# All of x ahead of the modulation pieces, filler matmuls around them, later query transposes in a two-layer mixer

## The chip, the cores and the metric

The kernel runs on one core of a Trainium2 chip. The metric is the device time of one execution in microseconds; lower is better.

## The reference

Two layers work on 256 latent tokens (x) and 256 context tokens, 2048 wide, in float32. Each layer computes shift, scale and gate from a conditioning vector, normalizes, projects, mixes in three ways, and adds the gated result:

```python
for l in range(2):
    shift, scale, gate = split(silu(c) @ ada_w[l] + ada_b[l], 3)        # 2048 -> 6144
    h = rmsnorm(x, norm_g[l]) * (1 + scale) + shift                     # context: its own vector c_ctx
    q, k, v, u_pool, u_fourier, g = split_proj(h @ w_in[l])             # 2048 -> 4608
    q = rope(rmsnorm(q)); k = rope(rmsnorm(k))                          # 8 query heads, 2 key heads
    mixed = concat(attention(q, k, v), pool(u_pool), fourier(u_fourier))
    x = x + gate * ((mixed * silu(g)) @ w_out[l])
return rmsnorm(x, final_norm_g)
```

## The kernel before

Tokens lie along the free dimension and channels along the partitions: x is loaded as 16 blocks of 128 channels by 512 tokens, in four groups of four blocks (`load_x`, L114). A large product in float32 is done by splitting both factors into a rounded part and a remainder (`split`, L137 to 139: ScalarE casts `hi`, VectorE subtracts for `lo`) and three matmuls of 512 columns (`mm3`). Weights come through three buffers of each of `raw`, `whi` and `wlo` (`wpiece`, L142), so a fourth weight piece waits until the first one's `lo` is made. All loads are issued on one queue, SP, in order.

**The startup** (`startup`, L838) makes the first layer's shift and scale and the normalized input `h` while the first weights arrive. The squares of x are made by ScalarE (three of four blocks) and VectorE (the fourth), summed in pairs by VectorE, and summed over channels by TensorE with a matrix of ones into two PSUM tiles (`stats`, eight matmul rows per half group). `norm` does the fourth group's `stats`, then the square root and the reciprocal (`rstd`). The modulation weights of layer 0 come in ten groups (`GROUPS`), for one or two channel blocks each, and each group in up to four pieces (`piece`, 512 KB or 1 MB, through four buffers). `ada_part` multiplies a piece with the conditioning vector, eight rows each; after the last piece of a group ScalarE copies the result (`ev`), TensorE transposes it, VectorE reduces it and makes `ab` and from it `h` (`make_h`). Behind each piece `work` issues matmuls of the projection from a list whose weights and `h` are there. `warm(n)` issues n float32 matmuls of ones with no use of the result (two rows each in the trace). TensorE's instructions in the startup stand in the order of the program. For the rest of the kernel, and for the other engines and SP, a planner orders the instructions by priority and by its own costs.

**The side work** (`Side`) interleaves attention with the projections: each generator yields a cost and a lag, `tick(0.64)` is called behind three matmuls, and a step is taken when the counted time has come. `q_prep` first makes the head norms and the rotary embedding of one 128-token block on VectorE, yields with a lag of 3.0, transposes the block's four heads on TensorE (L525), and goes on to the next block. It is added with a delay of `LAG_E` = 5.6 after each of the two query chunks of a layer, with `attention` behind it.

Of the kernel before, what the change touches and what calls it, by code (L numbers as in the profile page):

```python
# [20 lines left out]
P = 128  # L21
# [25 lines left out]
LAG_S, LAG_T, LAG_E, LAG_Q = 4.3, 1.4, 5.6, 0.0  # L47
# [9 lines left out]
def backbone(  # L57
# [24 lines left out]
    V, S, G, PE = nc.vector, nc.scalar, nc.gpsimd, nc.tensor  # L82
# [13 lines left out]
    def name(s):  # L96
        count[0] += 1
        return f"{s}_{count[0]}"
# [7 lines left out]
    def smt():  # L106
        return sm.tile([P, 512], F32, tag="sm", name=name("sm"))
# [6 lines left out]
    def load_x(g, n):  # L114
        for j in range(0, 4, n):
            nc.sync.dma_start(xk[g][:, j : j + n], xT[:, 4 * g + j : 4 * g + j + n])

    idt = const.tile([P, P], F32, name="idt")
    ones = const.tile([P, P], F32, name="ones")
# [17 lines left out]
    def split(src, hi, lo):  # L137
        i = S.copy(hi, src)  # L138
        V.tensor_sub(lo, src, hi.bitcast(F32))  # L139
        return i  # L140
# [143 lines left out]
    side = Side()  # L284
# [86 lines left out]
    def f4(s, shape, dt=F32R):  # L371
        return late["f4"].tile(list(shape), dt, tag="f4", name=name(s))
# [145 lines left out]
    def q_prep(qraw, qT, rq):  # L518
        rq.append(head_rstd(qraw, 4, P ** -0.5))
        for tt, r in qraw:  # L520
            qo = rope_one(tt, r, 4, 0)
            yield 0.0, 3.0 if tt == 0 else 1.0
            tp = smt()
            for hh in range(4):
                PE.transpose(tp[:, hh * P : hh * P + P], qo[:, hh], idt)  # L525
            c = slice(tt * P, tt * P + P)
            split(tp.rearrange("p (h n) -> p h n", h=4), qT[0][:, :, c], qT[1][:, :, c])
            yield 0.43, 0.0
# [47 lines left out]
    def layer(l, h, xs, chunk0):  # L576
# [62 lines left out]
        for g in range(2):  # L639
            accs = b_chunk(l, 3 + g, h, ntt, FILL[l][2])  # L640
            qraw = evac_raw(accs)
            if l == 0:
                side.finish("a0")
                qT = pair8(4, (T,))
            else:
                qT = [a.rearrange("p a (b n) -> p (a b) n", b=2) for a in pair8(2, (2 * N,))]
            rq = []
            side.add(f"q{g}", q_prep(qraw, qT, rq), LAG_E, "k")
            for qt in range(ntt):
                side.add(f"a{g}", attention(g, qt, qT, rq, kT, vv, mixed, off), 0.0, f"q{g}")  # L650
        korder = list(range(8, 16)) + list(range(8))
# [48 lines left out]
        k = KT - 1  # L700
        ws = [wpiece(wo[k, half], (P, 8, P)) for half in range(2)]
        for s in range(2):
            a = mmt()
            c = slice(s * N, s * N + N)
            for half, (hi, lo) in enumerate(ws):
                for j in range(8):
                    kk = korder[half * 8 + j]
# [121 lines left out]
            V.scalar_tensor_tensor(th, th, 1.0, g, op0=ALU.add, op1=ALU.mult)  # L829
        return th  # L830

    for g in range(3):
        load_x(g, 2)
    cq = [f4("cq", (P, 2, 512), F32) for _ in range(2)]
    h0 = H(T, "h")

# [1 line left out]
    def startup():  # L838
        st = tc.tile_pool(name="st", bufs=ST)
        with st as st:  # L840
# [14 lines left out]
            def stats(g):  # L855
                q = [t2("sq") for _ in range(4)]
                for j in range(4):
                    x = xk[g][:, j]
                    if j == 3:
                        V.tensor_mul(q[j], x, x)  # L860
                    else:
                        i = S.activation(q[j], x, AF.Square)
                        if g == 0 and j == 0:
                            tc.add_manual_dep(
                                i.ins, root.ins.name, mybir.DependencyInfo(mybir.DependencyClass.NoSync, mybir.DependencyReason.DATA)
                            )
                    if j % 2:
                        V.tensor_add(q[j - 1], q[j - 1], q[j])
                pairs = [(o, c, j) for o, c in zip(ss, halves) for j in (0, 2)]
                for o, c, j in pairs if g == 3 else sorted(pairs, key=lambda e: e[2]):  # L870
                    PE.matmul(o[:, :N], ones, q[j][:, c], start=g == 0 and j == 0, stop=g == 3 and j == 2)
# [3 lines left out]
            def norm():  # L875
                stats(3)
                for o, c in zip(ss, halves):
                    S.activation(rstd[:, c], o[:, :N], AF.Sqrt, bias=epst, scale=1.0 / D)
                for c in halves:
                    V.reciprocal(rstd[:, c], rstd[:, c])  # L880
                V.tensor_scalar(adab[:, KT : 2 * KT], adab[:, KT : 2 * KT], 1.0, None, op0=ALU.add)

            first = [mmt() for _ in range(4)]
            early = {}
            gfirst = [smt() for _ in range(NE)]
# [64 lines left out]
            start = [sum(GROUPS[:j]) * P * 4096 for j in range(len(GROUPS))]  # L950
# [28 lines left out]
            def ada_part(a, raw, kk, first_, last, w_):  # L979
                for i in range(4):  # L980
                    PE.matmul(  # L981
                        a[32 * i : 32 * i + 32, :w_], cs[:, 4 * kk + i], raw[:, i], start=first_, stop=last, tile_position=(0, 32 * i)
                    )

            def warm(n):
                for _ in range(n):
                    PE.matmul(first[3][:, :P], ones, ones, start=True, stop=True)

            with tc.manual_schedule(engines={mybir.EngineType.PE}):
                for g in range(3):  # L990
                    stats(g)
                for j, gs in enumerate(GROUPS):
                    a = smt()
                    w_ = 256 * gs
                    npc = 4 - ND[j]
                    raws = []
                    for kk in range(npc):
                        if j == 0 and kk == 1:
                            load_x(3, 1)
                        if j == 1 and kk == 3:  # L1000
                            late["store"]()
                        if kk == npc - 1 and j + 1 < len(GROUPS):
                            dvec(j + 1)
                        raws.append(piece(j, kk))
                        now[0] = 4 * j + kk + 4 - npc
                        if kk + 4 - npc == (PFK if j else 3):
                            queue(4 * j + 4 + (QK if j else Q0), k0, gs)
                        if j == 0 and kk == 2:
                            norm()
                        if j == 0 and kk == 3:  # L1010
                            nc.sync.dma_start(idt, ident)
                        ada_part(a, raws[kk], kk, kk == 0, kk == npc - 1, w_)
                        if j == 1 and kk < 2:
                            warm(3 - 2 * kk)
                        work(RATE * gs // 2)
                    with tc.high_priority(offset=CHAIN if j == 0 else 0):
                        ev = t2("ev")
                        S.copy(ev[:, :w_], a[:, :w_])
                        if j:
                            work(4)  # L1020
                        else:
                            warm(3)
                        for q in range(2 * gs):
                            PE.transpose(a[:, q * P : q * P + P], ev[:, q * P : q * P + P], idt)
                        if j:
                            work(4)
                        else:
                            store_cb(cvk, a[:32, 2 * P : 3 * P])
                            warm(2)
                        red = sp.tile([P, 2, gs, 2], F32, tag="red", name=name("red"))  # L1030
                        V.tensor_reduce(
                            red.rearrange("p w k v -> p (w k) v"), a[:, :w_].rearrange("p (q g r) -> p q r g", g=4, r=32)[:, :, 0:2, :],
                            axis=AX.X, op=ALU.add,
                        )
                        dst = ab[0][:, :, k0 : k0 + gs]
                        bias = adab[:, : 2 * KT].rearrange("p (w k) -> p w k", w=2)[:, :, k0 : k0 + gs]
                        for e in range(ND[j]):
                            V.tensor_add(red, red, abq[:, e, :, k0 : k0 + gs])
                        V.tensor_add(dst, red, bias.unsqueeze(3).to_broadcast([P, 2, gs, 2]))
                        V.tensor_mul(dst[:, 1], dst[:, 1], ng[:, k0 : k0 + gs].unsqueeze(2).to_broadcast([P, gs, 2]))  # L1040
                        for i in range(gs):
                            k = k0 + i
                            for vs in ((0,), (1,)) if k == 0 else ((0, 1),):
                                make_h(h0, k, xk[k // 4][:, k % 4], rstd, 0, vs)
                    k0 += gs
                now[0] = 10 ** 6
                work(LATE)
                pool_tables(0)
                fourier_loads(0)
                work(10 ** 6)  # L1050
                rope_tables(0)
# [131 lines left out]
```

## Time and profile before

| what | us |
|---|---|
| median of 3 runs (1071.56 to 1074.11) | 1073.24 |
| profiled execution, its own time | 1073.19 |
| its span, first to last instruction | 1071.4 |
| TensorE busy in the span | 1047.4 |
| VectorE busy | 842.3 |
| ScalarE busy | 479.7 |

Between the span and the execution's own time lie 1.8 us. Busy time of TensorE counts matmuls from issue to a modelled end, so a full row of it can still hide matmuls further apart than they need be. Times in the rows are microseconds from the start of the span. A chain of waits is followed back from the last instruction: at each step to what released it.

### The profile page before, as it was taken

To read this page: it belongs to the slowest core of one execution; us is meant where nothing else is said; L and a number is where in the kernel's file an instruction comes from. 1 tells how busy PE (TensorE), PEld (TensorE's weight loads), DVE (VectorE), ACT (ScalarE), POOL (GpSimd) and SP (SyncE) were. 2 spreads that over 40 slices of the span, in tenths; PEclk is the share of its full clock that TensorE was granted. 3 is DMA by queue.
4 is the path that set the end of the run, shared out by engine and by line. 5 is a ranking of instruction groups with operands and counts; after the bars stand their busy time and mean duration, and the time that the engine had idled before them with its cause. 6 is when DMAs were issued, how large, how long until landed. Compare 5 with 4: busy or idle time off the path is not lost.

```text
span 1071.4 us, 14049 instructions
## 1 busy us (share of the span) xinstructions
PE 1047.4 (98%) x5100; PEld 842.6 (79%) x5100; DVE 842.3 (79%) x1553; ACT 479.7 (45%) x803; POOL 0.2 (0%) x4
## 2 busy tenths in 40 slices
PE   6899999999999999999999999999999999999996
PEld 4466677888787888888888888887888888888885
DVE  6358648998999779998989787489657889776565
ACT  5233225323323766632522223288326767447453
POOL 0000000000000000000000000000000000000000
PEclk9999999999999999999999999999999999999999
DMA  8999777566785244457776667445764565686563
GB/s 336 410 398 343 256 238 242 164 198 214 227 260 169 80 140 158 157 192 273 266 272 213 197 195 265 139 133 169 271 218 161 168 196 185 224 270 212 192 201 117
DMA packets 63797, 233.63 MB, mean 218 GB/s; under 512 B 7104, under 2 KB 8176, under 8 KB 60016
## 3 DMA queue, kind: packets, MB, share of 16 engines
q1 hardware_dynamic: 63152, 231.69, 63.8%
q10 hardware_dynamic: 576, 1.05, 0.3%
q8 instruction: 40, 0.66, 0.3%
q14 instruction: 29, 0.24, 0.1%
HBM read 230.58 MB, written 2.12 MB: 217 GB/s over the span
## 4 chain that ended last, share of the span: by engine, by line
PE 81%; DVE 7%; DMA 4%; ACT 3%; issue 3%; SPq 0%; DVEq 0%; ACTq 0%
PE mm L336 18%; PE mm L335 18%; PE mm L337 18%; PE mm L932 6%; PE mm L311 5%; PE sm L932 3%; DVE ajunk L188 2%; DMA a<-in_ada 2%; PE mm L312 2%; PE sm L336 2%; PE sm L337 2%; PE sm L335 2%; PE sm L981 2%; DVE wlo L139 2%; PE sm L562 1%
## 5 line engine op out<-in xcount | busy, mean ns | idle before, releaser
L138 ACT CAST whi<-raw 128x1024 fp32r<-128x1024 f32 (+1 forms) x216 | 219.9, 1019 | 333.0 <-PE mm L336 112.1
L139 DVE TENSOR_TENSOR wlo<-raw,whi 128x1024 fp32r<-128x1024 f32 (+1 forms) x216 | 255.3, 1182 | 103.7 <-ACT whi L138 102.6
L188 DVE SCALAR_TENSOR_TENSOR ajunk<-araw,cbt 128x1024 bf16<-128x1024 f32 x224 | 273.6, 1221 | 49.8 <-DMA araw<-in_adar 36.9
L335 PE MATMUL mm<-whi,h 128*128 128x512 f32 x416 | 167.6, 403 | 0.0
L336 PE MATMUL mm<-wlo,h 128*128 128x512 f32 x416 | 163.3, 393 | 0.0
L337 PE MATMUL mm<-whi,h 128*128 128x512 f32 x416 | 163.1, 392 | 0.0
L335 PE MATMUL mm<-m,whi 128*128 128x512 f32 (+1 forms) x272 | 102.6, 377 | 0.0
L336 PE MATMUL mm<-m,whi 128*128 128x512 f32 (+1 forms) x272 | 102.4, 377 | 0.0
L337 PE MATMUL mm<-m,wlo 128*128 128x512 f32 (+1 forms) x272 | 102.4, 377 | 0.0
L311 PE MATMUL mm<-h,whi 128*128 128x512 f32 x256 | 92.5, 400 | 0.0
L337 PEld LDWEIGHTS mm<-whi,h 128*128 128x128 f32 x416 | 78.1, 188 | 17.0 <-DVE h L139 0.3
L336 PEld LDWEIGHTS mm<-wlo,h 128*128 128x128 f32 x416 | 78.2, 188 | 16.2 <-issue 1.9
L335 PEld LDWEIGHTS mm<-whi,h 128*128 128x128 f32 x416 | 78.2, 188 | 16.1 <-issue 1.7
L335 PE MATMUL mm<-h,whi 128*128 128x512 f32 x196 | 77.7, 396 | 0.0
L337 PE MATMUL mm<-h,wlo 128*128 128x512 f32 x196 | 76.8, 392 | 0.0
L336 PE MATMUL mm<-h,whi 128*128 128x512 f32 x196 | 76.8, 392 | 0.0
L312 PE MATMUL mm<-h,wlo 128*128 128x256 f32 x256 | 72.4, 283 | 0.0
L932 PE MATMUL mm<-whi,h 128*128 128x512 f32 x192 | 63.8, 401 | 0.2 <-ACT h L138 0.2
L335 PEld LDWEIGHTS mm<-m,whi 128*128 128x128 f32 x272 | 51.2, 188 | 9.5
L337 PEld LDWEIGHTS mm<-m,wlo 128*128 128x128 f32 x272 | 51.2, 188 | 9.4
L336 PEld LDWEIGHTS mm<-m,whi 128*128 128x128 f32 x272 | 51.2, 188 | 9.2
L311 PEld LDWEIGHTS mm<-h,whi 128*128 128x128 f32 x256 | 48.1, 188 | 10.8
(229 smaller groups left out, 1639.1 us busy)
## 6 DMA issues: line engine op xcount, KB each, us to landing
araw<-in_adar SPq DMA_DIRECT2D x128, 512.0 KB, 4.0
raw<-in_wb SPq DMA_DIRECT2D x78, 512.0 KB, 3.6
raw<-in_wg SPq DMA_DIRECT2D x55, 512.0 KB, 4.3
a<-in_ada SPq DMA_DIRECT2D x24, 1024.0 KB, 9.1
raw<-in_wo SPq DMA_DIRECT2D x32, 512.0 KB, 4.3
raw<-in_wot SPq DMA_DIRECT2D x32, 512.0 KB, 3.9
a<-in_ada SPq DMA_DIRECT2D x16, 512.0 KB, 4.6
x<-in_xT SPq DMA_DIRECT2D x4, 1024.0 KB, 8.1
```

What stands on the lines that cost most here:

```text
L138: i = S.copy(hi, src)
L139: V.tensor_sub(lo, src, hi.bitcast(F32))
L188: V.scalar_tensor_tensor(junk, raw, 1.0, cbt[:, v], op0=ALU.mult, op1=ALU.mult, accum_out=acc[:, u, h, v : v + 1])
L311: PE.matmul(a.rearrange("p (s n) -> p s n", s=2), hi[:, j - j0], h.both[k][:, :, :N], start=s0, stop=False)
L312: PE.matmul(a[:, :N], lo[:, j - j0], h.hi[k][:, :N], start=False, stop=s1)
L335: PE.matmul(o, ah, bh, start=start, stop=False)
L336: PE.matmul(o, ah, bl, start=False, stop=False)
L337: PE.matmul(o, al, bh, start=False, stop=stop)
L562: PE.transpose(tp[:, h * P : h * P + P], ps[h][:, i * P : i * P + P], idt)
L932: PE.matmul(o, lt, r, start=s0, stop=s1)
L981: PE.matmul(a[32 * i : 32 * i + 32, :w_], cs[:, 4 * kk + i], raw[:, i], start=first_, stop=last, tile_position=(0, 32 * i))
```

## The change

`load_x` is called for the fourth group too (in four transfers, as before) ahead of the startup, and no longer behind the first modulation piece. On TensorE ten fillers stand ahead of the first `stats`, `norm` stands behind the three `stats` and ahead of all pieces, and two fillers stand behind each of the first three pieces. The fillers write to the first gate tile in place of a projection tile. The delay of the first layer's `q_prep` is 7.1 in place of 5.6.

```diff
@@ layer
-            side.add(f"q{g}", q_prep(qraw, qT, rq), LAG_E, "k")
+            side.add(f"q{g}", q_prep(qraw, qT, rq), LAG_E + (1.5 if l == 0 else 0.0), "k")
@@ ahead of startup
-    for g in range(3):
-        load_x(g, 2)
+    for g in range(4):
+        load_x(g, 2 if g < 3 else 1)
@@ startup
             def warm(n):
                 for _ in range(n):
-                    PE.matmul(first[3][:, :P], ones, ones, start=True, stop=True)
+                    PE.matmul(gfirst[0][:, :P], ones, ones, start=True, stop=True)
 
             with tc.manual_schedule(engines={mybir.EngineType.PE}):
+                warm(10)
                 for g in range(3):
                     stats(g)
+                norm()
                 for j, gs in enumerate(GROUPS):
                     a = smt()
                     w_ = 256 * gs
                     npc = 4 - ND[j]
                     raws = []
                     for kk in range(npc):
-                        if j == 0 and kk == 1:
-                            load_x(3, 1)
                         if j == 1 and kk == 3:
                             late["store"]()
...
-                        if j == 0 and kk == 2:
-                            norm()
                         if j == 0 and kk == 3:
                             nc.sync.dma_start(idt, ident)
                         ada_part(a, raws[kk], kk, kk == 0, kk == npc - 1, w_)
+                        if j == 0 and kk < 3:
+                            warm(2)
                         if j == 1 and kk < 2:
                             warm(3 - 2 * kk)
```

## Rows read from the trace of the kernel before

**Rows 1.** The page: busy us of each engine; GB/s in 40 slices.
```profile
PE 1047.4 (98%) x5100; PEld 842.6 (79%) x5100; DVE 842.3 (79%) x1553; ACT 479.7 (45%) x803; POOL 0.2 (0%) x4
...
GB/s 336 410 398 343 256 238 242 164 198 214 227 260 169 80 140 158 157 192 273 266 272 213 197 195 265 139 133 169 271 218 161 168 196 185 224 270 212 192 201 117
```

**Rows 2.** The chain of waits, 0 to 50 us: start, duration, what.
```profile
8.93 7.83 DMA a<-in_ada
...
19.04 2.87 DVE rstd L880 x2
...
26.66 7.67 DMA a<-in_ada
...
35.50 11.06 DMA a<-in_ada
```

**Rows 3.** Windows: busy us (count) of each engine, granted clock, DMA share, GB/s.
```profile
21.00:24.00 3.00, 3.00 (x33) 1.92 (x31) 3.00 (x8) 1.08 (x3) 0.00 (x0) 1.00 1.03 403
24.00:27.00 3.00, 2.77 (x18) 1.54 (x17) 2.32 (x6) 1.35 (x3) 0.00 (x0) 1.00 0.57 136
...
480.00:500.00 20.00, 20.00 (x90) 16.58 (x89) 17.71 (x26) 4.14 (x5) 0.00 (x0) 1.00 0.74 248
```

**Rows 4.** Timeline of SP, 20 to 28 us: start, duration, instruction, count.
```profile
20.37 0.43 SPq L145 DMA_DIRECT2D raw<-in_wb  x1
23.91 0.33 SPq L145 DMA_DIRECT2D raw<-in_wgs  x1
...
24.77 2.96 SPq L976 DMA_DIRECT2D a<-in_ada  x4
```

**Rows 5.** SP's waits, 15 to 30 us: total, times, longest.
```profile
SPq L145 <- DVE wlo L139: 3.0, 1, 3.0
```

**Rows 6.** Timeline of TensorE, VectorE and ScalarE, 7 to 25 us.
```profile
7.73 1.22 PE L871 MATMUL sm<-sq,ones 128*128 128x256 f32 x2 [7.73 <-DVE sq L868]
...
10.45 1.06 PE L871 MATMUL mm<-sq,ones 128*128 128x256 f32 x2
...
14.96 0.59 PE L871 MATMUL mm<-sq,ones 128*128 128x256 f32 x2
...
16.29 0.69 DVE L868 TENSOR_TENSOR sq<-sq,sq 128x512 f32<-128x512 f32 x1
...
17.36 1.13 PE L871 MATMUL sm<-sq,ones 128*128 128x256 f32 x4
...
19.29 1.07 PE L981 MATMUL sm<-a,cs 128*32 128x256 f32 x16
20.29 0.94 PE L987 MATMUL mm<-ones 128*128 128x128 f32 x6
...
20.70 0.62 ACT L138 CAST whi<-raw 128x512 fp32r<-128x512 f32 x1
...
21.93 0.64 PE L981 MATMUL sm<-a,cs 128*32 128x256 f32 x8
22.32 0.11 DVE L1031 TENSOR_REDUCE red<-sm 128x4 f32<-128x16 f32 x1
22.50 0.94 PE L987 MATMUL mm<-ones 128*128 128x128 f32 x6
...
23.16 0.68 DVE L139 TENSOR_TENSOR wlo<-raw,whi 128x512 fp32r<-128x512 f32 x1
23.36 0.64 PE L981 MATMUL sm<-a,cs 128*32 128x256 f32 x8
...
24.66 0.50 PE L932 MATMUL mm<-whi,h 128*128 128x512 f32 x1 [0.23 <-ACT h L138]
```

**Rows 7.** TensorE's waits, 20 to 50 us.
```profile
PE sm L981 <- DMA a<-in_ada: 2.3, 3, 1.2
```

**Rows 8.** Timeline of VectorE and TensorE around the first query transposes.
```profile
335.40 0.68 DVE L491 TENSOR_TENSOR qo<-qo,tm 128x512 f32<-128x512 f32 x1
...
336.23 0.63 PE L525 MATMUL sm<-idt,qo 128*128 128x128 f32 x4 [1.00 <-DVE nt L235]
```

## The prediction

> **What bounds the kernel now.** I read the page first. TensorE is busy for 1047.4 of 1071.4 us, so 24 us are all that better ordering can win, the wait for the first data and the tail included; the DMA row is high in the first three of its slices (26.8 us each) and already lower in the first, 336 GB/s against 410 in the second [rows 1]. A stretch of the middle shows TensorE full without a gap: 90 matmuls in 20 us, 0.222 us each [rows 3]. What the change touches early is therefore worth what it takes out of the first 50 us, and that shift is kept afterwards.
>
> Then the chain of waits up to 50 us [rows 2]. It goes through the transfers: piece 1 of the modulation weights lands at 8.93 + 7.83 = 16.76; the two reciprocals of the row norms follow; then, over the SP queue, two pieces issued at 26.66 and 35.50, which land at 34.33 and 46.56. Beyond 46.56 TensorE is the chain. So up to there the stream of transfers sets the time, and the question is where it has a hole. The windows show it: 403 GB/s at 21 to 24 us, 136 at 24 to 27 [rows 3]. Lost: 3 x (1 - 136/403) = 2.0 us.
>
> Why the hole: SP issues a weight piece at 20.37 and nothing more until 23.91, and the other pieces only from 24.77 [rows 4]. The view of SP's waits says for what: 3.0 us for `wlo`, the VectorE half of splitting the first weight piece, whose buffer is to be reused [rows 5]. ScalarE's half was done at 20.70 + 0.62 = 21.32, but VectorE sat in the reciprocals from 19.04 and came to `wlo` at 23.16 [rows 2, 6]. The late norm closes SP, and SP's order puts everything behind it.
>
> **The change, part by part. (1) x ahead of piece 0.** The fourth group of x has four transfers of 256 KB and passes one piece of 512 KB: 0.524 MB / 403 GB/s = 1.30 us (estimate from the rate of [rows 3]). Its last quarter landed one piece before piece 1, at 16.76 - 1.30 = 15.46; it will land near 14.2. Pieces 1 to 3 have the same bytes ahead of them as before, so they land as before: 16.76, 18.06, 19.36; piece 0 lands 1.3 us later, at 15.5. No bytes are added.
>
> **(2) The norm ahead of the pieces.** On TensorE the fourth `stats` now stands before piece 0. Its last VectorE sum ended at 16.29 + 0.69 = 16.98, 1.5 us after the last landing [rows 6]; now 14.2 + 1.5 = 15.7. Six of its eight matmuls need it: of the 1.93 us from 17.36 to 19.29 that is 1.5 us, so piece 0 begins at 17.2 instead of before the norm. If ScalarE's squares are held by a buffer it is up to 0.6 later (the step from x's landing may not shrink at all); I take 17.2 and keep 17.8. The first half of the norm is ready near 16.1 instead of 18.5, so the reciprocals run from about 16.6 to 20.0.
>
> **(3) The fillers.** `warm(10)` is 20 rows in a stretch where TensorE has no data; even at twice 0.11 us each, 4.4 us in all, it fits ahead of the first squares at 7.73 [rows 6], so it costs nothing. The three `warm(2)` do cost. A piece alone takes 22.50 - 21.93 = 0.57; `warm(3)` behind a piece 23.36 - 22.50 = 0.86, so `warm(2)`, with two rows of 0.11 fewer, about 0.64 [rows 6]. Four pieces and three fillers: 4 x 0.57 + 3 x 0.64 = 4.2, so piece 3 ends at 21.4, against 20.29 before: 1.1 us later, and nothing waits for a transfer there, since piece 3 landed at 19.36. Behind it stands the unchanged row of fillers, transposes and two pieces, 20.29 to 24.42. The first real matmul stood at 24.66, of which 0.23 was a wait for `h` [rows 6]; it now comes at 21.4 + 4.13 = 25.5, 0.9 us later. `h` is no longer late: xn is multiplied beforehand, and reduce, add, scale and cast follow the transposes by about 1.5 us.
>
> **(4) What the early norm gives back.** VectorE is free at 20.0, so `wlo` can follow `whi` at 21.3 and end at 22.0 instead of 23.84; SP goes on 1.9 us sooner, and the hole closes but for a tenth of a us. TensorE is 0.9 us late at 25 us but then waited for pieces: 2.3 us in all from 20 to 50 us [rows 7]. With the stream 1.9 us earlier these waits go: -2.3 + 0.9 = -1.4. The stream itself allows -1.9; TensorE's own order is the smaller gain, and I take -1.5, between them. Bounds: -2.0 (the hole), and +0.9 if `wlo` keeps its place behind the reduce of the late piece, since then the hole stays and TensorE's 0.9 is the loss.
>
> **(5) Query transposes 1.5 us later.** In the first layer's first query group TensorE waited 1.0 us at the transposes: VectorE's last rotary sum ran at 335.40 for 0.68 us, and the transposes came at 336.23 [rows 8]. The planner counts 0.64 us for three matmuls, so 1.5 us is two or three turns, six to nine matmuls of 0.222 = 1.3 to 2.0 us of work put ahead of them. That covers 1.0. The preparation on VectorE is planned later by the same 1.5 us, but its order there need not move. I take -1.0; bounds -1.0 and 0 (the preparation slips behind another 1.2 us operation). The second group and the later attention show no such wait in the view of TensorE's waits, so the delay costs nothing there.
>
> Sum: 1073.19 (the profiled execution; the median is 1073.24, the same) - 1.5 - 1.0 = **1070.7 us**, 0.24% less. What a measurement here can tell from no change is about 0.2%, 2.1 us, so 1071.1 is the border.
>
> **A rule against it.** The first stats pairs took 1.06 us, the later ones 0.59 [rows 6], and at 21 us the granted clock reads 1.00 [rows 3]: TensorE began at the 1.2 GHz level and went to 2.4 GHz in its first unbroken run, between 10.45 and 14.96. The Trainium skill (TensorE: Matmul & The Clock Gate, Part 1) says the array starts throttled, is released by sustained work and falls back after idling. By that rule, `warm(10)` followed by a wait for data may release nothing, and norm and pieces, now with gaps, could run at the lower level, which would make the sum that of rival (c), 1076.2, in place of 1070.7. The trace agrees with the release, and shows no fall behind its waits of up to 1.2 us [rows 7].
>
> **Rivals.** *(a) The hole stays.* If `wlo` is still planned behind the reduce, SP stays shut until about 24, and the late piece 3 (+0.9) is on the path: 1073.19 + 0.9 - 1.0 = 1073.1. For it: `wlo` did stand behind the reduce of 22.32 [rows 6]; against: the reduce is later now and the norm earlier, so VectorE would idle with `wlo` ready. *(b) Only the start works.* The query preparation slips with its transposes: 1071.7. For it: VectorE's sum ended only 0.15 us before the transposes [rows 8], so any later start is felt. *(c) Half rate in the pieces,* the side of a loss. If TensorE is at the lower level from `stats` 3 on, six stats rows cost 0.21 more (1.3), four pieces two waves of 0.21 (1.7), three and two fillers, 22 rows, 0.11 (2.4): 5.4 us. With 0.9 that is 6.3 late; 2.3 of waits absorb, +4.0. With the hole's gain then worthless and the queries' 1.0: 1073.19 + 4.0 - 1.0 = 1076.2. For it: the first pairs' 1.06; against: TensorE is busy from its first microseconds on now, and before it reached the upper level within 7.2 us of its first matmul, 14.96 - 7.73 [rows 6]. It decides once the clock costs more than the 1.4 us of part 4. *(d) More goes than I count:* the fillers fall into waits, and small waits of TensorE elsewhere (about 1 us) go with the new order: 1073.19 - 2.0 - 1.0 - 1.0 = 1069.2. *(e) No effect at all:* reads moved inside a full stream, the stall merely moved: 1073.2.
>
> **Chances.** Forecast 0.45; (a) 0.18; (b) 0.15; (c) 0.08; (d) 0.08; (e) 0.06. The forecast's own range is 1069.7 to 1071.8 and lies beyond the border three times in four; (b) once in four. Faster by over 0.2%: 0.34 + 0.04 + 0.08 = 0.46. Slower (above 1075.4): 0.07. Within: 0.47. The range leaves out most of (c) and half of (d): 1069.2 to 1074.2.
>
> **What would show it.** The fourth x group lands near 14.2 and the reciprocals start near 16.6 (part 1, 2). Piece 3's matmuls end near 21.4 and the first matmul on `h` stands near 25.5 (part 3): if earlier, the fillers lie in waits. SP shows no pause of 3 us after 20.4 and the window 24 to 27 reads near 400 GB/s (part 4); the landing that stood at 46.56 comes near 45. No wait at the first query transposes near 334 (part 5). I am wrong if the hole is still there, if the stats pairs after 13 us take 1.06 again, or if an operation far from these places opens a new wait.

## The result: 0.5% slower

The changed kernel takes **1078.07 us** (median of 6, 1076.88 to 1080.39), the kernel before 1073.28 in the same series: ratio 1.005, 95% interval 1.0035 to 1.0066. Forecast were 1070.7 us and a gain. The profiled execution took 1079.56 us; the rows below are of it.

The page of the changed kernel: busy us of each engine, GB/s in 40 slices, and the queue of TensorE's instruction fetches (packets, MB, share).

```profile
PE 1056.4 (98%) x5132; PEld 848.8 (79%) x5132; DVE 842.7 (78%) x1553; ACT 479.4 (44%) x803; POOL 0.2 (0%) x4
...
GB/s 339 419 365 351 246 240 245 168 197 204 222 259 183 81 135 145 149 182 256 265 273 223 206 197 262 139 127 188 266 211 168 156 198 188 238 259 212 184 211 113
...
q8 instruction: 40, 0.66, 0.2%
```

TensorE has 32 more matmul rows than in [rows 1], all in the start-up; no other engine has more work. The prediction did not use the last line, and it turns out to matter.

Windows of the changed kernel, columns as in [rows 3].

```profile
21.00:24.00 3.00, 3.00 (x33) 2.14 (x26) 1.05 (x6) 1.56 (x4) 0.00 (x0) 1.00 0.99 327
24.00:27.00 3.00, 3.00 (x22) 1.88 (x20) 1.91 (x6) 1.35 (x3) 0.00 (x0) 1.00 0.83 272
...
45.00:50.00 5.00, 4.05 (x19) 0.96 (x20) 2.48 (x6) 2.07 (x3) 0.00 (x0) 0.66 1.03 416
...
395.00:400.00 5.00, 4.48 (x13) 3.11 (x14) 3.33 (x5) 4.91 (x12) 0.00 (x0) 0.71 0.74 226
```

The hole in the stream is not closed but spread: 327 and 272 GB/s against 403 and 136. And in two places far from the start-up the granted clock stands below 1.00.

SP of the changed kernel: timeline, then its wait, as in [rows 4, 5].

```profile
17.81 0.33 SPq L976 DMA_DIRECT2D a<-in_ada  x1
...
20.61 0.43 SPq L145 DMA_DIRECT2D raw<-in_wb  x1
23.75 0.33 SPq L145 DMA_DIRECT2D raw<-in_wgs  x1
...
24.60 1.37 SPq L976 DMA_DIRECT2D a<-in_ada  x3
```

```profile
SPq L145 <- DVE wlo L139: 2.6, 1, 2.6
```

SP opens at 23.75 instead of 23.91. The first of these lines is the fifth modulation piece; in the kernel before it stood 1.6 us earlier:

```profile
16.18 0.33 SPq L976 DMA_DIRECT2D a<-in_ada  x1
```

It needs the buffer of piece 0, which is now multiplied behind the norm (17.11 below, 15.48 before). TensorE and VectorE in the start-up, as in [rows 6], show why:

```profile
8.30 1.06 PE L871 MATMUL mm<-sq,ones 128*128 128x256 f32 x2
...
11.56 0.59 PE L871 MATMUL mm<-sq,ones 128*128 128x256 f32 x2
...
17.11 0.64 PE L981 MATMUL sm<-a,cs 128*32 128x256 f32 x8
...
20.75 0.64 PE L981 MATMUL sm<-a,cs 128*32 128x256 f32 x8
...
25.23 0.47 PE L932 MATMUL mm<-whi,h 128*128 128x512 f32 x1
...
16.86 3.36 DVE L880 RECIPROCAL rstd<-rstd 128x256 f32<-128x256 f32 x2 [1.30 <-ACT rstd L878]
...
22.90 0.17 DVE L1031 TENSOR_REDUCE red<-sm 128x4 f32<-128x16 f32 x1 [1.88 <-ACT crow L157]
22.99 0.68 DVE L139 TENSOR_TENSOR wlo<-raw,whi 128x512 fp32r<-128x512 f32 x1
```

The reciprocals run 2.2 us earlier (16.86 against 19.04), but `wlo` still stands behind the reduce of the late piece: VectorE idles 1.88 us ahead of that reduce, with `wlo` behind it in its queue.

TensorE's waits in the changed kernel (total, times, longest), at 20 to 50, 50 to 330 and 330 to 445 us.

```profile
PE sm L981 <- DMA a<-in_ada: 2.8, 3, 1.7
...
PE mm L335 <- DVE vl L139: 1.3, 1, 1.3
...
PE sm L562 <- ACT p L550: 0.9, 1, 0.9
PE sm L335 <- ACT p L545: 0.5, 1, 0.5
```

Laid over the trace of before, matmul for matmul, the changed kernel is 0.4 us ahead at 40 us, 1.7 behind at 50, 2.8 behind at 260, 6.4 behind at 480 and at the end. So the loss of 6.4 us in the span arises mainly in three places: +2.1 at 40 to 50, +1.3 at 240 to 260, +3.5 at 320 to 480; none is one of the places that the prediction summed over, except the last. The first place shows in the landings of the modulation pieces: up to the one at 41.23 us (41.55 before) they are 0.3 us ahead; the next, issued at 33.54 in both kernels, lands at 45.26 instead of 44.05, and the one behind it at 47.76 instead of 46.56.

### The profile page after: what moved, and what is told of

It is laid out like the page before. It is cut to its first block, busy times and chain, and to the rows that moved or that the text cites. A ratio compares the mean times of both kernels' runs of the same rounds, so it can differ in the third digit from the quotient of the medians.

```text
span 1077.8 us, 14117 instructions
## 1 busy us (share of the span) xinstructions
PE 1056.4 (98%) x5132; PEld 848.8 (79%) x5132; DVE 842.7 (78%) x1553; ACT 479.4 (44%) x803; POOL 0.2 (0%) x4
## 4 chain that ended last, share of the span: by engine, by line
PE 81%; DVE 7%; DMA 4%; issue 3%; ACT 3%; SPq 0%; DVEq 0%; ACTq 0%
PE mm L335 18%; PE mm L336 18%; PE mm L337 18%; PE mm L932 6%; PE mm L311 5%; PE sm L932 3%; DVE ajunk L188 3%; PE mm L312 2%; PE sm L981 2%; DMA a<-in_ada 2%; PE sm L335 2%; PE sm L336 2%; PE sm L337 2%; DVE wlo L139 1%; PE sm L562 1%
```

## Which half of the change costs the time

The start-up part and the query delay share no instruction, so each was run alone, and the start-up part also without its fillers between the pieces.

**e1_start**: the changed kernel without the query line. **e2_query**: the kernel before with the query line alone. **e3_query_short**: the same with 0.7. **e4_start_no_fill**: e1_start without the three pairs between the pieces.

```diff
 # e1_start, against the changed kernel
-side.add(f"q{g}", q_prep(qraw, qT, rq), LAG_E + (1.5 if l == 0 else 0.0), "k")
+side.add(f"q{g}", q_prep(qraw, qT, rq), LAG_E, "k")
 # e3_query_short, against e2_query
-LAG_E + (1.5 if l == 0 else 0.0)
+LAG_E + (0.7 if l == 0 else 0.0)
 # e4_start_no_fill, against e1_start
-                        if j == 0 and kk < 3:
-                            warm(2)
```

> The startup part alone (x ahead, norm ahead, fillers), the query delay as before. Theory Q, the loss is in the query delay: the startup changes little, 1073.0 to 1075.0 (the profile of the changed kernel is 1.7 us late at 100 us, part of which may be chance: two pieces landed 1.2 us late there and the clock fell for 3.4 us). Theory S, the startup is the loss (fillers on TensorE's path, half clock): 1076 to 1078.

> The query delay alone, startup as before. Theory Q: the wait of 1.0 us at the first transposes goes, but the attention steps of group 0 that are left at the end of the next chunk are forced without their lags, TensorE waits there and its clock falls: 1076 to 1078 (+3 to +4.5). Theory S: 1072.2 (-1.0), as predicted.

> Before with 0.7 us of query delay in the first layer in place of 1.5. Theory Q by dose: one turn of delay; if the loss grows with the number of steps left at the chunk's end, between 1072.0 and 1075.5, less than the run with 1.5. Theory S: 1072.2 to 1072.7.

> The startup part without the three times two fillers between the first pieces, query delay as before. If the fillers are on TensorE's path and it matters, 1 to 2 us less than the run with the startup part alone; if the transfers set the end there, or if the fillers keep the clock up, the same or up to 2 us more.

Measured, against 1072.42 us for the kernel before: e1_start 1077.24 (ratio 1.0037, 1.0025 to 1.005), e2_query 1074.62 (1.002, 1.0011 to 1.0029), e3_query_short 1073.66 (1.0007, 0.9998 to 1.0016), e4_start_no_fill 1072.35 (1.0001, 0.9993 to 1.001). Neither theory had the time of e2_query, and e4_start_no_fill gave back more than the 1 to 2 us expected. Both halves lose; x and the norm ahead of the pieces gain nothing and cost nothing; the six filler matmuls between the pieces cost 4.9 us by the medians, 3.9 by the ratios, although with them the first real matmul stands only 0.6 us later than before (25.23 against 24.66 [rows 6]). With 0.7 in place of 1.5 the delay leaves the wait of [rows 8] in the trace and still gains nothing.

## The fillers: path or count

The pairs add six matmuls to TensorE's path and also 24 rows (each filler matmul is two matmuls and two weight loads in the trace) to its program. Crossing the two: **e5_count** has the six ahead of the statistics, where TensorE is idle, and none between the pieces; **e6_path** keeps the pairs between the pieces and takes six away ahead of the statistics.

```diff
 # e5_count, against e4_start_no_fill
-                warm(10)
+                warm(16)
 # e6_path, against e1_start
-                warm(10)
+                warm(4)
```

> Start-up part alone, with the six matmuls of the three filler pairs moved ahead of the statistics (sixteen there, none between the pieces): as many TensorE instructions as in e1_start, but nothing added to TensorE's path between the pieces. Theory P (the pairs cost by standing on TensorE's path between the pieces): as e4_start_no_fill, ratio 1.000, 1072.4 us (1071.8 to 1073). Theory F (the pairs cost because added instructions move TensorE's instruction fetches onto stretches in which weights are waited for): most of e1_start's loss stays, 1075 to 1077 us, ratio 1.0025 to 1.004, with a step of the shift at 160 to 180 and at 245 to 260 us of the trace.

> Start-up part alone, with the three filler pairs between the pieces kept and four matmuls instead of ten ahead of the statistics: the instruction count of e4_start_no_fill, the path of e1_start. Theory P: as e1_start, 1077 us (1076 to 1078), ratio 1.0035 to 1.0045. Theory F: only what the pairs themselves take ahead of the first real matmul stays, about 0.9 to 1.3 us, 1073.3 to 1073.7 us, ratio 1.001, and no step of the shift at 160 to 180 us.

e5_count took 1075.53 us (1.0031, 1.0019 to 1.0042), e6_path 1073.22 (1.0008, 1.0 to 1.0017): most of the loss goes with the count (2.7 us by the medians), little with the path (0.4 by the medians, 0.9 by the ratio).

What moves with the count is the instruction fetch of TensorE, queue 8 in the DMA view. It brings 0.66 MB in 40 packets, 16 KB each, one about every 25 us; 2 x 5132 rows by 40 are 257 rows a packet. The Trainium skill (Runtime: NRT & Kernel Launch, Instruction fetch mechanics) gives blocks of 16 KiB, 256 instructions; the trace agrees. That page of the Trainium skill calls the cost of a block's boundary "mostly hidden"; the rows below show one in the loads beside it. The DMA view of e5_count at 165 to 166 us (packets, MB, share of 16 engines), and there and at 243.7 us the time from issue to landing:

```profile
q8 instruction: 1, 0.02, 6.5%
...
raw<-in_wb SPq DMA_DIRECT2D x1, 512.0 KB, 6.1
...
cbt<-cd SPq DMA_DIRECT2D x1, 512.0 KB, 7.5
```

The same two loads in e4_start_no_fill, whose fetches fall at 172.7 and 247.7 us:

```profile
raw<-in_wb SPq DMA_DIRECT2D x1, 512.0 KB, 4.2
...
cbt<-cd SPq DMA_DIRECT2D x1, 512.0 KB, 5.4
```

In this 1 us the fetch took as much as one of the 16 DMA engines for 6.5% x 16 x 1 us = 1.04 us. The trace holds sixteen completion times for a load, and the landing is the last of them. e4_start_no_fill is the low end of what is seen without a fetch: in the kernel before, where none falls beside it either, the first load took

```profile
raw<-in_wb SPq DMA_DIRECT2D x1, 512.0 KB, 5.2
```

Over the fifteen traces without a fetch beside it, this load took 4.1 to 5.4 us, over the five with one 4.8, 5.0, 5.4, 6.1 and 6.5; the second took 5.4 to 6.9 us in the eleven without, 5.6 to 7.5 in the nine with one. So a fetch doesn't always delay a load, but e5_count's two, e1_start's 6.5 and 7.1, and the second of the changed kernel with 7.4 lie outside of what is seen without one. What the second late load does, on VectorE and TensorE of e5_count:

```profile
251.32 1.23 DVE L188 SCALAR_TENSOR_TENSOR ajunk<-araw,cbt 128x1024 bf16<-128x1024 f32 x1 [1.90 <-DMA cbt<-cd]
...
257.42 0.41 DVE L139 TENSOR_TENSOR vl<-mm,vh 128x256 fp32r<-128x256 f32 x1
...
257.88 0.50 PE L335 MATMUL mm<-h,whi 128*128 128x512 f32 x1 [1.35 <-DVE vl L139]
```

and the first of these in e4_start_no_fill:

```profile
247.19 1.23 DVE L188 SCALAR_TENSOR_TENSOR ajunk<-araw,cbt 128x1024 bf16<-128x1024 f32 x1 [0.78 <-DMA cbt<-cd]
```

VectorE waits 1.90 us instead of 0.78 for the broadcast; that sum, three more of 1.2 us and a `wlo` stand ahead of `vl` in its queue, and TensorE stands 1.35 us; in e4_start_no_fill it does not stand there. Matmul for matmul, e5_count loses to e4_start_no_fill 0.3 us by 160, 1.8 at 160 to 180 and 2.1 at 240 to 260, which is nearly all of the 4.3 us between the profiled executions.

If it is the moment of the fetches, more instructions may cost less. **e9_after_four**: the changed kernel with `warm(4)`. **e10_count22**, **e11_count28**: e5_count with 22 and 28. **e12_before_count**: the kernel before with sixteen ahead of its statistics and nothing else.

```diff
 # e9_after_four, against the changed kernel
-                warm(10)
+                warm(4)
 # e10_count22 and e11_count28, against e5_count
-                warm(16)
+                warm(22)    # e11: warm(28)
 # e12_before_count, against the kernel before
-                    PE.matmul(first[3][:, :P], ones, ones, start=True, stop=True)
+                    PE.matmul(gfirst[0][:, :P], ones, ones, start=True, stop=True)
+                warm(16)
                 for g in range(3):
                     stats(g)
```

> The changed kernel whole, with four matmuls instead of ten ahead of the statistics, so that TensorE executes as many instructions as in e4_start_no_fill and e6_path; fillers between the pieces and the query delay stay. Theory F (the loss of the pairs is one of instruction count: where TensorE's instruction fetches fall): about 3.8 us under the changed kernel, as e6_path under e1_start; 1073.8 to 1075.3 us, ratio 1.0015, what is left being the query delay's. Theory P (path): as the changed kernel, 1077 to 1078 us.

> e5_count with 22 matmuls instead of 16 ahead of the statistics, where TensorE is idle: a larger count still, nothing on the path. Theory F (position of the fetches): the fetch near 42 us comes some microseconds earlier still and the one near 166 too, so they leave the places where weights are late; the time is not a rising line in the count, and either this kernel or e11_count28 is back within 1.5 us of e4_start_no_fill, 1072.4 to 1074. Theory Q (each instruction added costs, wherever it stands): 1.2 us less or more for each two added as between ten and sixteen, so 1078 to 1079 us here.

> e5_count with 28 matmuls ahead of the statistics. Theory F: as for e10_count22, no rising line; 1072.4 to 1076 us. Theory Q: 1081 to 1082 us.

> The kernel before with sixteen matmuls ahead of the statistics and nothing else: x, the norm and the query transposes stand where they stood. Theory F (count alone, whatever the order of the loads): the fetches fall as in e5_count, near 21, 42 and 166 us, and the time is 1075 to 1077 us, ratio 1.0025 to 1.004. Rival O (the count is harmful only with x loaded ahead and the norm ahead of the pieces): 1072 to 1073.5 us.

Then, to separate the places and to follow the changed kernel itself: **e13_count_late** adds the six at 45 us, behind the moment near 42; **e16_after_sixteen** and **e17_after_28** are the changed kernel with 16 and 28 ahead.

```diff
 # e13_count_late, against e4_start_no_fill
+                        if j == 3 and kk == 0:
+                            for _ in range(6):
+                                PE.matmul(a[:, :P], ones, ones, start=True, stop=True)
                         ada_part(a, raws[kk], kk, kk == 0, kk == npc - 1, w_)
 # e16_after_sixteen, against the changed kernel
-                warm(10)
+                warm(16)    # e17: warm(28)
```

> e4_start_no_fill with six more matmuls of the filler's size at 45 us, where TensorE waits 1.1 us for a modulation piece: the count of e5_count from there on, so the fetch that e4_start_no_fill has near 48 us stays about there and the later ones fall near 165, 195 and 249 us, as in e5_count. Theory F1 (the loss arises where fetches meet the weight and broadcast transfers at 165 to 172 and 243 to 251 us): 1074.3 to 1076 us, ratio 1.002 to 1.003, with late landings of the wb load issued at 165 us (over 5 us) and of the second cd broadcast issued near 243 us (over 6.5 us). Rival F2 (the loss is one of the start-up's pieces alone): 1072.0 to 1073.2 us.

> The changed kernel whole with sixteen matmuls instead of ten ahead of the statistics, so the count of e10_count22, fillers between the pieces and query delay kept. Theory F: more instructions, yet 3.5 to 4.5 us under the changed kernel, as e10_count22 under e5_count: 1073.5 to 1075 us, ratio 1.001 to 1.002, what is left being the query delay. Theory P (path) or Q (each instruction costs): 1078 us or more.

> The changed kernel whole with 28 matmuls instead of ten ahead of the statistics; fillers between the pieces and query delay kept. Theory F, by moments (a fetch at 41 to 42 us is what costs): twelve more than e16_after_sixteen bring the fetch to about 39 us and the one after 150 us to about 160; 1073.5 to 1075.3 us, ratio 1.001 to 1.002. Rival G (fillers between the pieces with more than ten instructions ahead cost whatever the moment): 1077.5 to 1079 us.

All kernels of this question, by the fetch nearest to 42 us in their traces. "Ahead + between" are filler matmuls that the kernel has ahead of the statistics and between the first pieces; q marks the query delay of the change; us are medians, and since the kernel before took 1072.4 to 1073.3 in the different series, the ratio is what compares.

| kernel | ahead + between | fetches near 42 and after 150 us | us | ratio (95%) |
|---|---|---|---|---|
| before | 0 + 0 | 50.3, 176.8 | 1073.24 | 1 |
| e4_start_no_fill | 10 + 0 | 48.6, 172.7 | 1072.35 | 1.0001 (0.9993 to 1.001) |
| e9_after_four | 4 + 6, q | 48.5, 171.5 | 1074.67 | 1.0016 (1.0007 to 1.0025) |
| e6_path | 4 + 6 | 47.8, 173.3 | 1073.22 | 1.0008 (1.0 to 1.0017) |
| e13_count_late | 10 + 0, 6 at 45 us | 47.0, 165.2 | 1075.04 | 1.0023 (1.0014 to 1.0032) |
| e5_count | 16 + 0 | 41.9, 165.6 | 1075.53 | 1.0031 (1.0019 to 1.0042) |
| e1_start | 10 + 6 | 41.9, 166.2 | 1077.24 | 1.0037 (1.0025 to 1.005) |
| e12_before_count | 16 + 0 | 41.6, 165.6 | 1078.14 | 1.0042 (1.003 to 1.0055) |
| e16_after_sixteen | 16 + 6, q | 41.3, 164.9 | 1078.22 | 1.0043 (1.003 to 1.0057) |
| changed kernel | 10 + 6, q | 41.0, 167.2 | 1078.07 | 1.005 (1.0035 to 1.0066) |
| e10_count22 | 22 + 0 | 39.7, 162.0 | 1072.17 | 0.9995 (0.9987 to 1.0004) |
| e11_count28 | 28 + 0 | 38.4, 159.4 | 1072.68 | 1.0 (0.9991 to 1.0009) |
| e17_after_28 | 28 + 6, q | 36.3, 157.4 | 1074.9 | 1.0028 (1.0016 to 1.004) |

The five kernels with a fetch between 41 and 42 us are the five slowest, the kernel before with nothing but sixteen idle-time matmuls among them; the interval of e5_count, the least of the five, overlaps those of e13_count_late and e17_after_28. With 22 or 28 the loss is gone, so added instructions do not cost by their number. The miss is e16_after_sixteen: counting alone I put its fetches where e10_count22 has them, but the fillers between the pieces set TensorE back by 1.4 us, and its fetch came at 41.3. So the theory was mended: the moment decides, and the count only through it. e17_after_28, whose expectation was written after that miss, came back to 1074.9, its ratio somewhat above the 1.002 expected; its fetches came 2 to 3 us earlier than forecast, at 36.3 and 157.4. The query delay alone has 1.002 (e2_query), so little is left for its start-up.

e13_count_late separates the places: no fetch comes near 42 us, and the one at 165.2 us comes as in e5_count; the one expected near 249 us came at 247.7, where e4_start_no_fill has it too. It lost 2.0 us, as theory F1 said, but its trace does not show where. The load issued at 165 us landed after 5.4 us:

```profile
raw<-in_wb SPq DMA_DIRECT2D x1, 512.0 KB, 5.4
```

That is no later than the same load can land without a fetch, and the second broadcast took 6.3 us instead of the more than 6.5 expected. The trace is of the fastest execution, 1073.5 us against a median of 1075.04.

By the times, then, the six matmuls cost about 2 us when they come behind the moment of 42 us, and up to 2 more when they come ahead of it. In the changed kernel a fetch at that moment and a late load stand together, in the DMA view at 41 to 42 us and for the piece issued at 35.1 us, which took 11.06 us before [rows 2]:

```profile
q8 instruction: 1, 0.02, 6.3%
...
a<-in_ada SPq DMA_DIRECT2D x1, 1024.0 KB, 12.6
```

Of its sixteen completion times fifteen lie between 45.18 and 46.17 us, and the last at 47.76; in the kernel before all sixteen lie between 46.01 and 46.56. In the eleven traces in which no fetch falls into its flight this piece takes 11.05 to 11.08 us each time, in the nine others 11.03 to 12.61. A longer flight alone is no loss: in e10_count22 it took 11.62 us but was issued at 34.81 and landed at 46.43; in the five slow kernels it landed at 47.3 to 48.0, in all others by 47.1. Over all twenty traces, beyond 55 us, a load with a fetch in its usual time of flight lands about 0.25 us later on the mean than the median of the same load without one, and by more than 1 us in about one case in ten, against one in fifty without a fetch.

## The query delay

[rows 8] belongs to group 0. **e14_q0** and **e15_q1** delay one group each; **e7_q_gate** and **e8_gate** put one gate tile ahead of the point where the rest of attention group 0 is issued without gaps, with and without the delay.

```diff
 # e14_q0 (e15_q1: g == 1), against the kernel before
-side.add(f"q{g}", q_prep(qraw, qT, rq), LAG_E, "k")
+side.add(f"q{g}", q_prep(qraw, qT, rq), LAG_E + (1.5 if l == 0 and g == 0 else 0.0), "k")
 # e8_gate, against the kernel before; e7_q_gate: the same and the query line of the change
             if l == 0:
+                if g == 1:
+                    gated(14, gate_evac(a_tile(wg[l, 14], h, list(range(KT)), nt, FILL[l][3]), nt))
+                    eg[14] = None
                 side.finish("a0")
```

> The kernel before with the query delay of 1.5 us and, in layer 0, one gate tile (number 14 of group 1) computed ahead of the point at which what is left of attention group 0 is issued without gaps. Theory T1 (the delay loses its time there, since the steps that it pushes to that point stand bare): the tile takes up the waits at 393 to 396 us, and the time is 1 us under e8_gate's, 1071.5 to 1073. Theory T2 (the loss is spread over the whole attention of layer 0, by the later order of all its steps): 1.5 to 2.2 us over e8_gate's, 1074 to 1075.

> The kernel before with the gate tile of e7_q_gate alone, without the delay: what the tile's move is worth by itself. Both theories: within 1 us of the kernel before, 1072.0 to 1073.5 us; the base for e7_q_gate.

> The kernel before with the query delay in layer 0 for the first query group alone. Theory T1 (the delayed steps of group 0 are what stands bare at the chunk's end): the wait of 1.0 us at 336 us goes, the waits near 356 and 393 us come, and the time is that of e2_query, 1074 to 1075 us. Theory T2 (both groups' delays cost about alike): 1073.4 to 1073.8 us.

> The kernel before with the query delay in layer 0 for the second query group alone. Theory T1: the wait at 336 us stays, nothing new waits at 393 us, 1072.3 to 1073.2 us. Theory T2: 1073.4 to 1073.8 us.

Measured: e14_q0 1075.33 us (1.0025, 1.0015 to 1.0036), e15_q1 1072.5 (0.9997, 0.9989 to 1.0006). The whole loss is group 0's. TensorE's waits at 330 to 445 us, e14_q0:

```profile
PE sm L562 <- ACT p L550: 0.9, 1, 0.9
PE sm L336 <- DVE ptl L139: 0.8, 1, 0.8
PE sm L335 <- ACT p L545: 0.5, 1, 0.5
```

and e15_q1, where the wait of [rows 8] stands as before:

```profile
PE sm L525 <- DVE nt L235: 1.0, 1, 1.0
```

The delay removes a wait of 1.0 us and opens three of 2.2 us together: one at the first scores behind the chunk, at 354 us, and two at 391 to 397 us, where the chunk of group 1 ends and `side.finish("a0")` issues what is left of group 0's attention with nothing between its steps. That is 1.2 us of the 2.3; where the rest lies the view of waits does not say. The gate tile helped little: e7_q_gate took 1074.18 us (1.0016, 1.0007 to 1.0025), e8_gate 1073.54 (1.0011, 1.0003 to 1.002). They are 0.6 us apart instead of 2.2, within the noise of either: with the tile the wait on `ptl` is gone, but the other two stay, and the tile alone costs 0.7. The theory that the forced end carries all of the loss is half right.

**e18_best** joins what did no harm: x and the norm ahead, 22 ahead of the statistics, none between, the delay for group 1.

```diff
 # e18_best, against e10_count22
-side.add(f"q{g}", q_prep(qraw, qT, rq), LAG_E, "k")
+side.add(f"q{g}", q_prep(qraw, qT, rq), LAG_E + (1.5 if l == 0 and g == 1 else 0.0), "k")
```

> What the experiments leave of the change: x ahead of the pieces, the norm ahead, 22 matmuls ahead of the statistics, none between the pieces, the query delay in layer 0 for the second group alone. If the small gains of e10_count22 (ratio 0.9995) and e15_q1 (0.9997) are real and add, ratio 0.9992, 1072.1 us; if they are noise, 1.000, 1072.9 us. No version that beats the kernel before clearly is expected.

1073.45 us (1.0008, 0.9998 to 1.0017): no version beats the kernel before.

## Why the prediction was wrong, step by step

**(1) x ahead of piece 0: right, and worth nothing.** The last quarter of x landed at 14.06 us (forecast near 14.2), piece 0 at 15.34 (15.5), piece 3 at 19.23 (19.36).

**(2) The norm ahead: right in time.** Piece 0 begins at 17.11 (forecast 17.2), the reciprocals at 16.86 (16.6).

**(3) The fillers: the step that failed most.** The price of their path came out: the first real matmul stands at 25.23 (forecast 25.5), and e6_path, with the pairs on the path, is 0.4 us slower by the medians and 0.9 by the ratio (forecast 0.9). For the first real matmul that is partly luck: without the pairs it stands at 25.56 in e4_start_no_fill, behind waits for pieces, and at 25.18 in e10_count22. What failed is the way of pricing a filler by the time that it takes, at nothing for those "where TensorE has no data": sixteen matmuls also shift every later instruction fetch. `warm(10)` alone did cost nothing, as the prediction says (e4_start_no_fill); sixteen cost 2.7 to 5.3 us (e5_count, e1_start, e12_before_count), against the 0.9 that the prediction has for all of them. The premise that the shift of the first 50 us is "kept afterwards", since "beyond 46.56 TensorE is the chain", failed with it. The chain of the kernel before leaves TensorE from 165.66 to 174.34 us, with

```profile
168.00 4.45 DMA raw<-in_wb
```

so there was a second place where loads have no slack, and e1_start lost 1.4 us there, matmul for matmul, and 0.9 at 240 to 260 us.

**(4) The hole: rival (a).** `wlo` kept its place behind the reduce, as that rival said, and SP opened 0.16 us earlier instead of 1.9. The forecast term of -1.5 came to nothing, and not by `wlo` alone. In e4_start_no_fill, with parts (1) and (2) and without the pairs, SP opens 1.0 us sooner (1.4 in e10_count22), and the hole at 24 to 27 us is mostly filled:

```profile
18.79 0.33 SPq L976 DMA_DIRECT2D a<-in_ada  x1
...
22.90 0.33 SPq L145 DMA_DIRECT2D raw<-in_wgs  x1
```

```profile
18.00:21.00 3.00, 2.70 (x37) 1.37 (x37) 3.00 (x2) 0.87 (x3) 0.00 (x0) 1.00 0.83 281
21.00:24.00 3.00, 2.49 (x25) 1.87 (x23) 2.85 (x10) 1.59 (x5) 0.00 (x0) 1.00 0.98 354
24.00:27.00 3.00, 2.44 (x18) 1.62 (x17) 1.00 (x3) 0.30 (x1) 0.00 (x0) 1.00 0.98 343
```

Yet it equals the kernel before, and its piece of 46.56 lands at 47.01. The stream has its hole at 18 to 21 us now, 281 GB/s where the kernel before has 391: the fifth piece is issued at 18.79 instead of 16.18, since the pieces give their buffers back behind the norm. Part (2) priced the norm ahead of the pieces for TensorE alone and left this wait out; rival (e), the stall merely moved, has it. The objection to (a) in the prediction, that VectorE would idle with `wlo` ready, is what happened, 1.88 us of it.

**(5) The query delay: sign wrong.** The wait went, as forecast. That the delay "costs nothing" in the second group and the later attention was read from a trace in which the steps were not yet late: it holds for the second group's own delay (e15_q1), not for the attention steps of group 0 that the first delay makes late. It costs 2.2 us by e2_query, all through group 0.

Sum as measured: the start-up +4.8 instead of -1.5, the queries +2.2 instead of -1.0; together 7.0, the changed kernel 4.8. By the ratios it is 0.37% and 0.2% against 0.5% (0.35 to 0.66), so the two add within the noise. **Rival (c)** had the sign, not the place: the pieces ran at the upper level (a piece took 0.57 us, as before, and the clock reads 1.00 from 12 to 30 us). But the clock did fall in the changed kernel, behind new waits: 0.66 at 45 to 50 us and 0.71 at 395 to 400, where the kernel before reads 1.00. Eight matmuls of a piece took 1.60 us at 47.8 us instead of 1.11 at 34.0. The same waits at 391 us in e14_q0 were followed by 1.00, so the waits alone don't fix it.

**The rule against it** is borne out in part. In the changed kernel the ten fillers run from 1.04 to 5.20 us and TensorE then waits 2.4 us; the clock reads 0.50 at 8 to 11 us, and the stats pairs take 1.06 us (8.30), as in the kernel before. At 11.56 they take 0.59, and the first pieces take 0.57 as before. In the kernel before the column reads 1.00 at 8 to 11 us although they take 1.06 there; that trace holds no clock record ahead of 12.6 us.

**What stays open.** That loads with a fetch beside them land later on the mean is shown by the landings in twenty traces, and that the time goes with the fetches' moments by thirteen kernels. That the fetch is what costs the time is argued from both: no run here moves a fetch without adding or removing instructions. Each kernel has one trace: a single late landing, and a single late share of a load, are also seen without a fetch, e12_before_count's and e13_count_late's traces are of their fastest executions and show less than their medians, and the size of the loss near 42 us, 0 to 1.5 us in the landings, is not settled. The clock is a rival for part of it. Between 40 and 50 us the changed kernel and e16_after_sixteen lose 2.1 and 2.3 us, and in both the clock falls there; e5_count, e1_start and e12_before_count lose 0.1 to 0.6, about as much as e10_count22 with 0.5. And kernels without the loss have single executions about 3 us longer at a lower clock (e10_count22 1075.69 us with a mean of 0.994, its others 1071.2 to 1072.5 with 0.997 or 0.998), though not each execution with a lower clock is longer (e4_start_no_fill 1073.04 with 0.994). How much of the loss comes through the clock, behind a late load or without one, no run separates.

## What to carry to other kernels

Where a kernel is at 98% of its bound, a filler is not priced by its own duration: count its instructions, look up in the trace where the instruction fetches fall, and see which loads with no slack they would come to stand beside. Time a change that adds idle-time instructions with a few more and a few fewer of them before believing its sign, in both directions. And a stall removed by delaying a step was paid here where the delayed chain had to end; look for that point first, for the buffers that a reordered engine gives back later, and for the in-order queue position of the operation that frees a buffer before counting on it being freed earlier.

## What the runs showed of the hardware

TensorE's instruction fetch is visible in the DMA view: packets of 16 KB, each taking about 1.0 us of one of the 16 engines' time. Two loads of 512 KB beside one landed after 6.1 and 7.5 us, against 4.1 to 5.4 and 5.4 to 6.9 in the traces without one; other loads beside one were not late. Sixteen small matmuls in otherwise idle time, 32 of 5132 rows, made a kernel of 1073 us 5.3 us slower, while 28 of them, with x ahead, cost nothing. I had expected neither.
